# Scaling the last token tile on another engine, writing it by an accumulating store, and moving two multiplications and two weight loads

## The chip, the cores and the metric

The kernel runs on one core of one Trainium2 chip. The metric is the device time of one execution in microseconds (us); lower is better.

## What is computed

One layer of a diffusion backbone over 512 latent tokens of width 1024, with 256 context tokens. Only the part around the change has to be followed:

```python
x = x + g1 * mixed                                   # attention done before
hx2 = modulate(rmsnorm(x, norm_ffn_g[l]), sh2, sc2)  # h * (1 + scale) + shift
x = x + g2 * hierarchical_moe(hx2, ...)              # top-1 group, top-2 experts of it, 16 experts
return rmsnorm(x, final_norm_g)
```

So a row of `hx2` is `x * rstd * gs + sh`, where `rstd` is one number for each token, `gs = (1 + scale) * norm_ffn_g` and `sh` one vector each for all tokens. The router takes its logits from `hx2`; each token then goes through two of sixteen experts (`w_gate`, `w_up`, `w_down`), whose weights are 96 MB in all.

## The kernel before

The 512 tokens are four tiles of 128 rows (`t` = 0 to 3). After attention, each tile goes through the same steps:

- `out_sums` (L1217): TensorE multiplies by the output projection, in halves of 512 columns.
- `rows_half` (L1228): VectorE adds the residual (L1235); ScalarE squares and sums (L1237); VectorE multiplies by `gs` into `h2s[t]` (L1238). The buffers of `h2s` have the tag `t1`, of which there are three; the first held a constant, so tile 3 writes into the buffer of tile 0 and has to wait until tile 0's store has landed.
- `turn_half` (L1240): TensorE transposes four blocks; ScalarE copies them out of PSUM (L1246).
- `factor` (L1248) makes `rstd` in four small steps on VectorE and a root on ScalarE (L97 to L110), and `tile_logits` (L1253) the router's logits.
- `tile_end` (L1256): VectorE computes `h2s * rstd + sh` over 128x1024 (L1257), and SyncE (SP) issues the store of those rows to `hx_d` in DRAM (L1258).

`route` (L1108) is a generator of router steps on VectorE. `before3` is its instance for tiles 0 to 2 and `last3` the one for tile 3; `next(before3)` puts one step into VectorE's order. Its last steps, `places` (L1186), make the one-hot matrix `oh` for the slots: for tiles 0 to 2 by six instructions on GpSimd (POOL, L1192), for tile 3 by one on VectorE (L1195). `slot_sums` (L1199) multiplies them on TensorE; `slot_rows` (L1205) turns the result into the index list `idx`. Then `gather(0)` (L1260), an indirect DMA issued by GpSimd, fetches expert 0's token rows from `hx_d` into `xg[0]`; it needs `idx` and all four stores to `hx_d`. While it is under way VectorE computes the gains (`shares`, L1161), TensorE makes the other slot sums, and every engine passes a branch for overfull experts (L1415), whose body is not entered here. With `xg[0]` there, `turn_x(0)` transposes it (L1519), `split` makes `xh` (L62), and the matmuls of the sixteen experts follow without a gap.

Order. Inside `with tc.manual_schedule(engines=...)` (L1285) the named engines keep the order of the program; there these are TensorE and VectorE. The other engines' instructions are put in order by the framework's own list scheduler, which may move an instruction far ahead: the two `memset`s of `xg` (L1303), written inside the block, run on GpSimd at 368 us.

Weight loads. `load_experts(n)` (L446) issues the next n loads of 1 MB on SP. A load waits for the landing of the second load before it, or, where `behind` is given, for that instruction's landing alone. In the block one load is issued ahead of `tile_end(3)` and one behind it (L1325 to L1327). The loads up to the 15th wait for `gather(0)` (L1353), those after for `gather(1)` (L1493).

Of the kernel before, what the change touches and what calls it, by code (L numbers as in the profile page):

```python
# [12 lines left out]
AF = mybir.ActivationFunctionType  # L13
OP = mybir.AluOpType
# [3 lines left out]
P = 128  # L18
# [20 lines left out]
def hybrid_kernel(tc, nc, x_k, x_q, ctx, cvec, w_mod_a, w_mod_b, b_mod_c, b_mod_r, g_ffn_row,  # L39
                  w_v, w_kv, w_ql, w_qk, g_q, g_kv, w_uq, w_ukv, rel, w_out_a, w_out_b, w_r, b_r,  # L40
                  w_gate, w_up, w_down, g_fin_row, cpk0, cpk, out):
    sy, ac, ve, pe, gp = nc.sync, nc.scalar, nc.vector, nc.tensor, nc.gpsimd

    def pool(name, bufs=1, side="left", space=None):
        kw = dict(name=name, bufs=bufs, reuse_waits="tile")
        if space is None:
            return tc.alloc_tile_pool(side=side, **kw)
        return tc.alloc_tile_pool(space=space, **kw)
# [158 lines left out]
    def bank4(*nums):  # L207
        return bank(*nums).rearrange("p (a b) -> p a b", a=4)
# [143 lines left out]
    for b in range(3):  # L352
        n = KB[b + 1] - KB[b]
# [41 lines left out]
    for c in range(2):  # L395
        for b0, n in ((0, 4), (4, 2)):
            tr = bank4(4, 5, 6)
# [7 lines left out]
    for b0, n in ((0, 4), (4, 2)):  # L405
        tr = bank4(4, 5, 6)
# [10 lines left out]
    for c in range(3):  # L417
        tr = bank4(4, 5, 6)
# [22 lines left out]
    def add_slots(pl_, n):  # L441
        slots_.extend((pl_, f"ew{len(slots_) + i}") for i in range(n))
# [3 lines left out]
    def load_experts(n, behind=None):  # L446

        for i in range(len(loads), min(len(loads) + n, len(order))):
            e, q = order[i]
            pl_, tag = slots_[cur[0] % len(slots_)]  # L450
            cur[0] += 1
            places_.append(cur[0] - 1)
            w = pl_.tile([P, 2048], F32, name="ew", tag=tag, bufs=1)
            ins = sy.dma_start(w, (w_gate, w_up, w_down)[q // 2][e, q % 2])

            n_ = 2 if i < FL else FLIGHT
            if behind or i >= n_:
                tc.add_manual_dep(ins.ins, behind or started[i - n_], mybir.DependencyInfo(
                    mybir.DependencyClass.Sync, mybir.DependencyReason.DATA), reason="in flight")
            started.append(ins.ins.name)  # L460
            loads.append(w)
# [359 lines left out]
    def tr_tile():  # L821
        return psC.tile([P, 4, P], F32, name="tr", tag="tr", bufs=2)
# [257 lines left out]
    gs = wp.tile([P, D], F32, name="gs")  # L1080
    sh = wp.tile([P, D], F32, name="sh")
# [6 lines left out]
    load_experts(M1 - R1 - LD)  # L1088
    ve.scalar_tensor_tensor(gs, gs, 1.0, gff, op0=OP.add, op1=OP.mult)
    hx_d = tc.dram_tile([T, D], F32, name="hx_d")  # L1090

    def logits(ht):

        pl_ = psC.tile([P, 4, P], F32, name="o", tag="o", bufs=1)
        for k in range(KT):
            pe.matmul(pl_[:, 0, 0:20], ht[:, k, :], wr[:, k, :], start=(k == 0), stop=(k == KT - 1))
        return pl_[:, 0, 0:20]
# [7 lines left out]
    h2s = []  # L1105
# [93 lines left out]
    def slot_sums(pq, oh, va, i, n_i, n_rows):  # L1199

        for n in range(8):
            pe.matmul(pq[0:n_rows, 0, i * NE:(i + n_i) * NE], oh[n], va[n][:, i:i + n_i].rearrange("p a e -> p (a e)"),
                      start=(n == 0), stop=(n == 7))

    def slot_rows(pq, idx_, n_rows):  # L1205
        ve.tensor_scalar(idx_[0:n_rows, 0, :], pq[0:n_rows, 0, 0:NE], float(T), None, op0=OP.add)
# [10 lines left out]
    def out_sums(t, hf, cs_=range(4)):  # L1217
        if t not in ys_:
            ys_[t] = halves(0)
        cs = slice(hf * 512, hf * 512 + 512)  # L1220
        for c in cs_:
            wh, wl = wos[c]
            mm3(ys_[t][hf], omh[:, c, t * P:(t + 1) * P], oml[:, c, t * P:(t + 1) * P], wh[:, cs], wl[:, cs],
                start=(c == 0), stop=(c == 3))

    sq, hts = {}, {}

    def rows_half(t, hf):  # L1228

        if hf == 0:  # L1230
            sq[t] = wp.tile([P, 2], F32, name="ssh", tag="ssh", bufs=2)
            h2s.append(wp.tile([P, D], F32, name="t1", tag="t1", bufs=3))
        cs = slice(hf * 512, hf * 512 + 512)
        xs = x1s[t][:, cs]
        ve.tensor_tensor(xs, xs, ys_[t][hf], op=OP.add)  # L1235
        junk = wp.tile([P, 512], BF16, name="junk", tag="junk", bufs=2)
        ac.activation(junk, xs, AF.Square, accum_out=sq[t][:, hf:hf + 1])  # L1237
        ve.tensor_tensor(h2s[t][:, cs], xs, gs[:, cs], op=OP.mult)  # L1238

    def turn_half(t, hf):  # L1240
        if hf == 0:
            hts[t] = wp.tile([P, KT, P], F32, name="ht", tag="ht", bufs=1)
        tr = tr_tile()
        for k in range(4):
            pe.transpose(tr[:, k, :], x1s[t][:, (hf * 4 + k) * P:(hf * 4 + k + 1) * P], ident)
        ac.copy(hts[t][:, hf * 4:hf * 4 + 4, :], tr)  # L1246

    def factor(t):  # L1248
        ss = wp.tile([P, 1], F32, name="ss", tag="ss", bufs=2)
        yield from rstd_steps(ss, sq[t][:, 1:2], D, 1, wp, sq[t][:, 0:1])  # L1250
        yield ss

    def tile_logits(t, l, ss):  # L1253
        ve.scalar_tensor_tensor(lg[:, t, :], l, ss, lsh, op0=OP.mult, op1=OP.add)

    def tile_end(t, ss):  # L1256
        ve.scalar_tensor_tensor(h2s[t], h2s[t], ss, sh, op0=OP.mult, op1=OP.add)  # L1257
        return sy.dma_start(hx_d[t * P:(t + 1) * P, :], h2s[t]).ins.name  # L1258

    def gather(e):  # L1260
        ins = gp.indirect_dma_start(out=xg[e % NX][slice(0, CAP), :], out_offset=None, in_=hx_d,  # L1261
                                    in_offset=bass.IndirectOffsetOnAxis(ap=idx[slice(0, CAP), 0, e:e + 1], axis=0),
                                    bounds_check=T - 1, oob_is_err=False)
        gathers.append(ins.ins.name)
# [3 lines left out]
    for t in range(2):  # L1268
        out_sums(t + 1, 0)
        out_sums(t + 1, 1)  # L1270
        rows_half(t, 0)
        rows_half(t, 1)
        turn_half(t, 0)
        turn_half(t, 1)
        *_, ss = factor(t)
        tile_logits(t, logits(hts[t]), ss)
        tile_end(t, ss)

    N1, NF, N2 = 1, 3, 2
    L1, L2 = 2, 2  # L1280
# [1 line left out]
    R4 = 2  # L1282
    pp3 = pq0[:, 3:4, :]
    before3, last3 = route(0, 3), route(3, 4)
    with tc.manual_schedule(engines={pe.engine, ve.engine}):  # L1285
        out_sums(3, 0)
        rows_half(2, 0)
        rows_half(2, 1)
        turn_half(2, 0)
        turn_half(2, 1)  # L1290
        *_, ss = factor(2)
        out_sums(3, 1, (0, 1))
        tile_end(2, ss)
        l = logits(hts[2])
        rows_half(3, 0)
        out_sums(3, 1, (2, 3))
        ona.release()
        omp.release()
        chp.release()
        xp = pool("xp")  # L1300
        xg = [xp.tile([P, D], F32, name=f"xg{i}") for i in range(NX)]
        for x_ in xg:
            gp.memset(x_, 0.0)  # L1303
        rng4 = pool("rng4")
        add_slots(rng4, 5)
        rng5 = pool("rng5")
        add_slots(rng5, R4)
        vq = pool("vq")
        oh = vq.tile([P, 8, CAP], F32R, name="oh")
        va = vq.tile([P, 8, 4, NE], F32R, name="va")  # L1310
        pos = vq.tile([P, 4, 2], F32, name="pos")
        aa = vq.tile([P, 4, 2, 4, 4], F32, name="aa")
        aall = aa.rearrange("p t a g i -> p (t a) (g i)")
        load_experts(L1)
        tile_logits(2, l, ss)
        for _ in range(N1):
            next(before3)
        rows_half(3, 1)
        turn_half(3, 0)
        turn_half(3, 1)  # L1320
        for n, s3 in enumerate(factor(3)):
            if n < NF:
                next(before3)
        l = logits(hts[3])
        load_experts(L2 - 1)  # L1325
        tile_end(3, s3)
        load_experts(1)  # L1327
        for _ in range(N2):
            next(before3)
        tile_logits(3, l, s3)  # L1330
        for _ in before3:
            pass
        for _ in last3:
            pass
        slot_sums(pq0, [oh[:, n] for n in range(8)], [va[:, n] for n in range(8)], 0, 1, CAP)
        slot_rows(pq0, idx, CAP)
        gather(0)
        pc = tr_tile()
        for t in range(4):
            pe.matmul(pc[:, 0, 0:NE], trb[:, 1, :], mh[:, t, :], start=(t == 0), stop=(t == 3))  # L1340
        count = cst.tile([P, NE + 1 + NB * NE], I32, name="count")
        ve.tensor_copy(count[:, 0:NE], pc[:, 0, 0:NE])
        ve.tensor_reduce(out=count[:, NE:NE + 1], in_=pc[:, 0, 0:NE], axis=AX.X, op=OP.max)
        shares()
# [314 lines left out]
    with tc.manual_schedule(engines={pe.engine, ve.engine, ac.engine}):  # L1659
# [19 lines left out]
        for n in range(8):  # L1679
            wh, wl = half(n)  # L1680
            for i in range(2):
                k = n % 4 * 2 + i
                cs = slice(i * 512, i * 512 + 512)
# [235 lines left out]
```

## Time and profile before

| | |
|---|---|
| device time, three runs | 733.8, 735.29, 735.91 us; median 735.29 |
| the profiled execution | 733.54 us |
| its span, first to last instruction | 731.8 us |
| TensorE busy | 698.1 us, 95% of the span |
| VectorE, ScalarE, GpSimd busy | 546.4, 447.7, 83.7 us |
| granted TensorE clock, mean | 0.983 of full |

All rows of the trace are from the one profiled execution; its times count from the first instruction. "Start, length, engine, line, operation, written tile, read tiles" is the order within a row, and what stands in brackets is how long the engine had been idle and what ended that. Lines are those of the kernel before.

### The profile page before, as it was taken

How to read it: one execution, taken by the hardware profiler on the slowest of the kernel's cores; microseconds unless marked ns; L12 is line 12 of the kernel's file. 1: busy time of each engine (PE TensorE's matmuls, PEld its weight loads, DVE VectorE, ACT ScalarE, POOL GpSimd, SP SyncE). 2: the span in 40 equal slices, each digit the busy share in tenths (PEclk: the TensorE clock that was granted, in tenths of full speed). 3: DMA queues.
4: the chain of work that ended last, by engine and by line, in shares of the span. 5: the costliest groups of instructions: out<-in, count | busy, mean ns of one | idle time of the engine just before them, and what ended most of it. 6: DMA issues, size and time to landing. Idle time of an engine off the chain costs nothing. (4 is left out here: it accounts for less than half of the span.)

```text
span 731.8 us, 10466 instructions
## 1 busy us (share of the span) xinstructions
PE 698.1 (95%) x3918; PEld 516.9 (71%) x3919; DVE 546.4 (75%) x749; ACT 447.7 (61%) x698; POOL 83.7 (11%) x56
## 2 busy tenths in 40 slices
PE   4999999999999999999999679999999999999995
PEld 3678997767765887868658557777777777777773
DVE  4572457766676795656536778999999999999996
ACT  6451355654555455646644377777777777777763
POOL 1010000000000000000010122222222222221310
PEclk9999999999999999999999769999999999999998
DMA  8931238555476821121179979999999999999673
GB/s 319 409 124 60 73 95 279 194 172 190 144 236 202 288 88 43 60 76 54 59 252 364 346 244 364 362 372 370 353 360 357 358 352 350 358 354 379 239 132 116
DMA packets 39336, 174.58 MB, mean 239 GB/s; under 512 B 5711, under 2 KB 7191, under 8 KB 26992
## 3 DMA queue, kind: packets, MB, share of 16 engines
q1 hardware_dynamic: 34880, 163.72, 61.4%
q0 software_dynamic: 4112, 10.06, 6.3%
q8 instruction: 32, 0.52, 0.3%
q14 instruction: 24, 0.20, 0.1%
q10 hardware_dynamic: 288, 0.08, 0.0%
HBM read 163.00 MB, written 14.79 MB: 243 GB/s over the span
## 5 line engine op out<-in xcount | busy, mean ns | idle before, releaser
L1376 DVE TENSOR_TENSOR el<-ew,eh 128x2048 fp32r<-128x2048 f32 (+1 forms) x106 | 220.6, 2087 | 17.3 <-ACT eh L1373 13.7
L1373 ACT CAST eh<-ew 128x1024 fp32r<-128x1024 f32 x190 | 190.1, 1050 | 43.9 <-PE s L59 29.4
L57 PE MATMUL s<-eh,xh 128*96 128x512 f32 x260 | 104.7, 403 | 1.1 <-ACT xh L62 1.1
L59 PE MATMUL s<-eh,xl 128*96 128x512 f32 x260 | 103.3, 397 | 0.0
L58 PE MATMUL s<-el,xh 128*96 128x512 f32 x260 | 102.8, 395 | 0.0
L1588 POOL DMA_INDIRECT ya_d<-yo,idx x14 | 45.5, 3251 | 140.7 <-DVE yo L1592 140.7
L59 PEld LDWEIGHTS s<-eh,xl 128*96 128x96 f32 x260 | 42.3, 163 | 19.3 <-DVE xl L63 0.7
L57 PEld LDWEIGHTS s<-eh,xh 128*96 128x96 f32 x260 | 42.4, 163 | 18.3 <-ACT xh L62 1.4
L58 PEld LDWEIGHTS s<-el,xh 128*96 128x96 f32 x260 | 42.5, 164 | 17.5 <-DVE el L1376 0.2
L57 PE MATMUL y<-eh,ghh 128*96 128x512 f32 x120 | 48.2, 401 | 0.0
L59 PE MATMUL y<-eh,ghl 128*96 128x512 f32 x120 | 47.3, 394 | 0.0
L58 PE MATMUL y<-el,ghh 128*96 128x512 f32 x120 | 47.2, 393 | 0.0
L470 DVE TENSOR_REDUCE nm<-s 128x1 f32<-128x768 f32 x32 | 30.5, 954 | 19.1 <-PE s L59 18.9
L57 PE MATMUL ps<-wh,hh 128*128 128x512 f32 (+2 forms) x128 | 43.9, 345 | 0.5 <-ACT hh L275 0.3
L59 PE MATMUL ps<-wh,hl 128*128 128x512 f32 (+2 forms) x128 | 43.5, 345 | 0.2 <-DVE hl L277 0.2
L58 PE MATMUL ps<-wl,hh 128*128 128x512 f32 (+2 forms) x128 | 43.4, 341 | 0.0
L1303 POOL MEMSET xg<- 128x1024 f32 x2 | 1.9, 954 | 322.1 <-DMA g<-mod_d 322.1
L57 PE MATMUL ps<-hh,wh 128*128 128x512 f32 (+1 forms) x96 | 36.4, 379 | 0.0
L946 ACT ACTIVATE pr<-s,nm 128x768 f32<-128x768 f32 x32 | 29.1, 908 | 9.8 <-DVE nm L470 9.6
L59 PE MATMUL ps<-hh,wl 128*128 128x512 f32 (+1 forms) x96 | 34.4, 359 | 0.0
L58 PE MATMUL ps<-hl,wh 128*128 128x512 f32 (+1 forms) x96 | 34.2, 357 | 0.0
L1261 POOL DMA_INDIRECT xg<-hx_d,idx x16 | 24.2, 1510 | 65.9 <-PE t L1519 46.7
(360 smaller groups left out, 1455.8 us busy)
## 6 DMA issues: line engine op xcount, KB each, us to landing
ew<-w_gate SPq DMA_DIRECT2D x32, 1024.0 KB, 8.6
ew<-w_up SPq DMA_DIRECT2D x32, 1024.0 KB, 8.0
ew<-w_down SPq DMA_DIRECT2D x32, 1024.0 KB, 9.4
raw<-w_mod_b SPq DMA_DIRECT2D x32, 512.0 KB, 3.8
wm<-w_mod_a SPq DMA_DIRECT2D x16, 512.0 KB, 10.8
raw<-w_qk SPq DMA_DIRECT2D x8, 512.0 KB, 3.4
raw<-w_v SPq DMA_DIRECT2D x4, 512.0 KB, 10.5
ya_d<-zero SPq DMA_DIRECT2D x8, 256.0 KB, 3.2
```

Of the source, the lines that this page charges most:

```text
L57: pe.matmul(ps, lh, rh, start=start, stop=False)
L58: pe.matmul(ps, lh, rl, start=False, stop=False)
L59: pe.matmul(ps, ll, rh, start=False, stop=stop)
L470: ve.tensor_reduce(out=nm, in_=s, axis=AX.X, op=OP.max, negate=True)
L946: ac.activation(pr, s, AF.Exp, bias=nm, accum_out=mla_ssum[h // 2][:, t, h % 2:h % 2 + 1])
L1261: ins = gp.indirect_dma_start(out=xg[e % NX][slice(0, CAP), :], out_offset=None, in_=hx_d, in_offset=bass.IndirectOffsetOnAxis(ap=idx[slic ...
L1303: gp.memset(x_, 0.0)
L1373: ac.copy(wh[:, cs], r[:, cs])
L1376: ve.tensor_tensor(wl[:, cs], r[:, cs], f(wh[:, cs]), op=OP.subtract)
L1588: gp.indirect_dma_start(out=ya_d, out_offset=bass.IndirectOffsetOnAxis(ap=idx[rows, 1, e:e + 1], axis=0), in_=yo[rows, :], in_offset=None, ...
```

## The change

1. `tile_end(3)` no longer runs on VectorE. ScalarE multiplies `h2s[3]` by `rstd` (an activation of kind Copy with a scale for each row, 128x1024), and GpSimd issues a DMA that adds the result onto what stands in `hx_d`.
2. What stands there is `sh`: a new store on SP writes `sh` into those 128 rows of `hx_d`, soon after `sh` is loaded.
3. The two multiplications by `gs` of tile 3 move from VectorE to GpSimd.
4. GpSimd joins the engines that keep the order of the program in the block. Its order there is: multiplication of the first half, the two `memset`s of `xg`, multiplication of the second half, the accumulating store, the six `oh` instructions, `gather(0)`.
5. The copy out of PSUM for the second half of tile 3's transposes moves from ScalarE to VectorE. One step of `before3` moves ahead of it, and two steps instead of three stand between the steps of `factor(3)`.
6. Instead of one weight load ahead of `tile_end(3)` and one after it, one load is issued, and it waits for the accumulating store's landing. The other joins the load that waits for `gather(0)`.

```diff
     hx_d = tc.dram_tile([T, D], F32, name="hx_d")
+    sy.dma_start(hx_d[3 * P:4 * P, :], sh)
...
-        ve.tensor_tensor(h2s[t][:, cs], xs, gs[:, cs], op=OP.mult)
+        (ve if t < 3 else gp).tensor_tensor(h2s[t][:, cs], xs, gs[:, cs], op=OP.mult)
...
-        ac.copy(hts[t][:, hf * 4:hf * 4 + 4, :], tr)
+        if t == 3 and hf:
+            ve.tensor_copy(hts[t][:, hf * 4:hf * 4 + 4, :], tr)
+        else:
+            ac.copy(hts[t][:, hf * 4:hf * 4 + 4, :], tr)
...
     def tile_end(t, ss):
+        if t == 3:
+
+            ac.activation(h2s[t], h2s[t], AF.Copy, scale=ss)
+            return gp.dma_start(hx_d[t * P:(t + 1) * P, :], h2s[t], accum_op=OP.add).ins.name
...
-    with tc.manual_schedule(engines={pe.engine, ve.engine}):
+    with tc.manual_schedule(engines={pe.engine, ve.engine, gp.engine}):
...
         turn_half(3, 0)
+        next(before3)
         turn_half(3, 1)
         for n, s3 in enumerate(factor(3)):
-            if n < NF:
+            if n < NF - 1:
                 next(before3)
         l = logits(hts[3])
-        load_experts(L2 - 1)
-        tile_end(3, s3)
-        load_experts(1)
+        load_experts(1, tile_end(3, s3))
```

`NF` is 3 and `L2` is 2.

## Rows read from the trace of the kernel before

**Rows 1.** First line; stretches: length, PE, PEld, DVE, ACT, POOL busy, clock, DMA share, GB/s

```profile
span 731.8 us, 10466 instructions
...
387.00:398.00 11.00, 11.00 (x63) 9.41 (x63) 10.09 (x25) 5.63 (x13) 0.00 (x0) 1.00 0.98 366
412.70:425.00 12.30, 3.87 (x30) 3.34 (x31) 7.62 (x38) 4.67 (x6) 4.42 (x8) 0.50 0.81 278
457.00:690.00 233.00, 233.00 (x1109) 165.73 (x1108) 221.08 (x142) 179.47 (x199) 58.80 (x24) 1.00 0.99 359
```

**Rows 2.** Timeline of VectorE, 407 to 416 us

```profile
407.28 0.69 DVE L1238 TENSOR_TENSOR t<-x,gs 128x512 f32<-128x512 f32 x1 [0.72 <-DMA hx_d<-t]
...
409.05 0.69 DVE L1235 TENSOR_TENSOR x<-x,s 128x512 f32<-128x512 f32 x1 [0.16 <-PE s L59]
...
410.38 0.15 DVE L97 TENSOR_SCALAR nww<-ssh 128x1 f32<-128x1 f32 x1
...
412.24 1.28 DVE L1257 SCALAR_TENSOR_TENSOR t<-t,ss,sh 128x1024 f32<-128x1024 f32 x1
...
414.94 0.25 DVE L1153 TENSOR_REDUCE pos<-pm 128x6 f32<-128x96 f32 x1
```

**Rows 3.** Timeline of GpSimd, and its queue's waits and landing of gather(0) (L1261)

```profile
415.38 3.30 POOL L1192 TENSOR_SCALAR oh<-ck,pos 128x96 fp32r<-128x96 f32 x6 [44.90 <-DVE pos L1153]
...
420.82 1.09 POOL L1261 DMA_INDIRECT xg<-hx_d,idx  x1 [2.14 <-DVE ex L1166]
...
L1261 POOLq EVENT_SEMAPHORE  x4: 17/901/4222, 415.6 to 422.3; - x4
...
DMA to landing us min/median/max: 4.1/4.1/4.1
```

**Rows 4.** Timeline, the steps from the index list to the experts' first matmul

```profile
419.42 0.17 DVE L1206 TENSOR_SCALAR idx<-x 96x16 int32<-96x16 f32 x1 [1.13 <-PE x L1202]
...
424.39 0.65 PE L1202 MATMUL x<-va,oh 128*96 128x48 f32 x3 [0.30 <-PEq L1415]
...
425.02 1.51 PE L1519 MATMUL t<-c,xg 96*128 96x96 f32 x8
...
426.83 0.78 ACT L62 CAST xh<-t 128x768 fp32r<-128x768 f32 x1
```

**Rows 5.** Timeline of SP's issues, 412 to 425 us

```profile
412.75 0.33 SPq L454 DMA_DIRECT2D ew<-w_up  x1
413.55 0.33 SPq L1258 DMA_DIRECT2D hx_d<-t  x1
415.20 0.33 SPq L454 DMA_DIRECT2D ew<-w_up  x1
424.91 0.34 SPq L454 DMA_DIRECT2D ew<-w_down  x1
```

**Rows 6.** Gather(1): its issue, its landing, and queues' packets and MB, 426:429, then 429:431.8

```profile
424.96 1.01 POOL L1261 DMA_INDIRECT xg<-hx_d,idx  x1 [3.05 <-DMA xg<-hx_d,idx]
...
DMA to landing us min/median/max: 6.8/6.8/6.8
...
q1 hardware_dynamic: 122, 0.95, 85.9%
q0 software_dynamic: 5, 0.02, 1.7%
...
q0 software_dynamic: 209, 0.51, 68.4%
```

**Rows 7.** Prices: two groups of GpSimd, landing of L1640's accumulating transfers, a pass of ScalarE

```profile
L1640 POOL DMA_DIRECT2D x<-ya_d x4 | 3.7, 1436 | 4.5 <-ACT eh L1373 4.5
L1303 POOL MEMSET xg<- 128x1024 f32 x2 | 1.9, 954 | 322.1 <-DMA g<-mod_d 322.1
...
DMA to landing us min/median/max: 5.6/8.4/11.3
...
L1373 ACT CAST eh<-ew 128x1024 fp32r<-128x1024 f32 x190 | 190.1, 1050 | 43.9 <-PE s L59 29.4
```

## The prediction

> **What bounds the kernel now.** I read the busy time by stretch first [rows 1]. From 457 to 690 us TensorE is busy for all of 233.00 us: whatever moves the start of the experts' matmuls moves the end by as much, and nothing behind it hides a delay. From 412.7 to 425 us TensorE has 3.87 us of work in 12.3 us at half the full clock: the routing of the last tile and the fetch of expert 0's rows, where the change lies. The profiled execution took 733.54 us for a span of 731.8, 1.75 us below the median of 735.29; I work out a shift on the profiled one and add it to the median.
>
> The timelines of that stretch show two strands. One is **VectorE's**: tile 3's residual sum at 409.05, the factor's steps from 410.38, `tile_end` for 1.28 us at 412.24, the positions ready at 415.19 [rows 2]; then GpSimd's six `oh` instructions, 3.30 us from 415.38 to 418.68 [rows 3], and the index list at 419.42 to 419.59, 0.74 us after GpSimd's last [rows 4]. The other is the **store** of tile 3's rows, issued at 413.55 between two weight loads [rows 5]. `gather(0)` needs both. GpSimd's queue waited 4.222 us, from 415.7 (just after the first of those events at 415.6), to 419.9, 0.3 us beyond the index list: the store came last, by that little. The gather's own row starts at 420.82, 0.9 us after the wait, and it lands 4.1 us later, at 424.9 [rows 3]. The transposes of `xg` start at 425.02, just as TensorE ends the other slot sums (424.39 + 0.65); `xh` follows at 426.83 [rows 4]. So both strands end within 0.2 us of each other, and a gain has to come in both.
>
> **The change, part by part.**
>
> *VectorE.* It loses two multiplications (0.69 us as in the row at 407.28) and `tile_end` (1.28), and gets a copy of 128x512 out of PSUM, which I price as the sum that reads PSUM in the same shape, 0.69 [rows 2]. Between the sum's end at 409.74 and `rstd` at 412.24 it then has as much to do as before: the multiplication goes, the copy comes, and the three route steps stay (one of them moves ahead of the copy). But the copy has to wait for TensorE's transposes, which wait for the sum themselves, and the moved step fills only part of that wait. I allow 0.4 us for the rest, an estimate between nothing and the 0.7 of a whole half-tile operation. So `rstd` is ready at about 412.65, but `tile_end` doesn't follow it: the positions, 2.95 us after `rstd` before (412.24 to 415.19), come 1.67 us after it, at about 414.35, 0.85 earlier.
>
> *GpSimd's multiplications.* The first waits, as VectorE did, for tile 0's store (407.28 [rows 2]). No row shows a product of two inputs on this engine. From below: a `memset` writes 1024 columns in 0.954 us, so 512 written take 0.48 [rows 7]; from above: an `oh` instruction takes 0.55 us for 96 columns (3.30 / 6 [rows 3]), which times 512/96 is 2.9, as if nothing of it were fixed. I take 1.25, nearer the `memset`, since it has length and width like the product, with two operands read besides. The GPSIMD Engine Reference of the Trainium skill (section 3.1) gives 4497 ns for such an addition of 2048 columns, from which an estimate for 512 is 1.12 us; by it the sum stays as it is. With 1.25 us each and the two `memset`s between (1.9 [rows 7]) GpSimd ends at 407.3 + 4.4 = 411.7, ahead of `rstd`. This costs nothing up to (412.65 - 407.3 - 1.9) / 2 = 1.7 us each. The cover is 0.95 us.
>
> *ScalarE* scales 128x1024 in the time of a copy of that shape, 1.05 us [rows 7]: 412.7 to 413.8. It is otherwise idle here.
>
> *The store's issue on GpSimd.* It stands ahead of the six `oh` in the fixed order: a wait for ScalarE here would hold them up, and with them the index list. Four accumulating transfers issued in a row (L1640) kept GpSimd busy for 3.7 us, 0.92 each [rows 7]: 413.85 to 414.8, against positions at 414.35. So `oh` runs from 414.8 to 418.1, 0.6 earlier than before, and the index list is there at about 419.0.
>
> *The store's landing.* The first of the L1640 transfers, of the same 512 KB but from DRAM into SBUF, landed 5.6 us after its start, the others later as they queued behind each other (median 8.4) [rows 7]. From below I take the gather's 4.1 [rows 3], from above the 8.4. I take 5.6, as the store is alone once the earlier loads are through: 413.85 + 5.6 = 419.45. Before, the wait ended at 419.9, so here 0.45 us is won.
>
> *Storing `sh` first* adds 0.5 MB to a stretch with DMA at 0.98 share and 366 GB/s [rows 1]: 1.4 us of transfer time. The loads there are wanted after 427 us, so that costs nothing in itself; but tile 0's store, and with it GpSimd's first product, may come up to 1.4 us later. The cover of 0.95 us takes most of that; 0.45 us stays as a bound.
>
> *The weight loads.* The one of 415.20 goes behind the gather, with the one that was issued there at 424.91 [rows 5]; both feed chunks far behind, and I put that at nothing. The one of 412.75 now starts at the store's landing, 419.5, so right ahead of `gather(0)`. For that there is a model in the trace: at 424.91 a load was issued on SP, and at 424.96 `gather(1)` started [rows 5, 6]. From 426 to 429 us the load's queue moved 0.95 MB and the gather's 0.02; from 429 to 431.8 the gather's moved 0.51. The gather landed after 6.8 us instead of 4.1 [rows 6]. The load was through 4.1 us after its issue (429 less 424.91), and the gather landed 2.75 us after that (431.75). Here the load is through at 419.5 + 4.1 = 423.6, and `gather(0)` lands at 426.35. Alone it would have landed 4.1 us after its start at 419.45 + 0.9 = 420.35, so at 424.45.
>
> *The sum.* The transposes start at 426.4 instead of 425.02 and `xh` 1.6 us after that, at 428.0 (before, 1.81 passed there, the last 0.3 beyond the end of the transposes, waiting for work of VectorE that now comes earlier). That is 1.1 us behind 426.83 [rows 4]: 734.6 us for the profiled execution, **736.4** for the median. About 0.3% (2.2 us) is what a measurement of this kernel can tell from no change; I expect a loss below that. With the store's landing taken at 4.1 us the load is through at 422.1 and the gather lands at 424.85: no change. With 8.4 all shifts by another 2.8 us: 3.9 us slower.
>
> **The rivals.**
>
> *The gather isn't held up, and the time falls.* It then lands at 424.45, and TensorE's other slot sums end 0.6 earlier too, at 424.4. Both strands gain, `xh` comes 0.6 us earlier: 734.7. For it: the load starts 0.9 us ahead of the gather's row, and a queue could have let the gather in between; against it, the 0.02 MB from 426 to 429 us [rows 6]. The page DMA: Bandwidth & Descriptors of the Trainium skill (section on queues, rings and completion order) says that each DMA engine goes round between the queues packet by packet; by that rule the gather would share the bandwidth and this rival would hold, and the trace does not agree in the one stretch that resembles it. A quarter.
>
> *GpSimd is too slow, and the time rises clearly.* It hangs on one number, the product's duration, and decides from 1.7 us on. At 2.9 us: 407.3 + 2.9 + 1.9 + 2.9 = 415.0; ScalarE ends at 416.2; the store lands at 416.25 + 5.6 = 421.85; the load behind it is through at 426.0, the gather lands at 428.75, and the shift is 3.5 us: 738.8. For it: the fixed order puts everything behind these products. The same page on GpSimd (section 8) says that the engine contends with VectorE's instructions of two inputs for SBUF; VectorE runs those all through this stretch. Against it: the spread of 0.48 to 2.9 lies mostly below 1.7 where the width of the `memset` counts. 15 in 100.
>
> *Nothing changes.* The store lands early (as with 4.1 above), or the two effects cancel, and what VectorE loses was not on the path, since GpSimd's `oh` waits for the store's issue: within 0.7 us of 735.3. 15 in 100.
>
> **How the numbers follow.** Forecast (736.4) 45 in 100, rivals 25, 15 and 15. The forecast's own range, from the landing's bounds, is 735.3 to 739.2, most of it below 737.5. Faster than 733.1 is only the far end of the first rival, and what I have not seen: 9 in 100. Slower than 737.5: the second rival with 15 and the forecast's tail with 7, so 22. Within: 69. The range of 8 in 10 reaches from 733.6, a little beyond the first rival, to 738.2, where most of the second is left out.
>
> **What the profile after would show.** The load behind the store between the landing and the gather, its bytes first, and a landing of `gather(0)` over 5 us: the forecast. A landing near 4 us: the first rival. GpSimd's products over 1.7 us, or ScalarE's scaling starting later than `rstd`: the second. Positions by 414.5 and the index list by 419.1 would show VectorE's part right. The forecast is wrong if the store lands much before 419, if SP's order moves other stores, or if the start of the experts' matmuls moves without moving the end.

## The result and the profile after

The changed kernel takes **740.73 us** (median of 6 executions, 738.92 to 743.45) beside 733.15 us for the kernel before (6 executions, 732.35 to 735.91). The ratio is **1.0090, 95% interval 1.0067 to 1.0114**: 6.6 us slower. Forecast were 736.4 us, a range up to 738.2 and no change that can be measured; the time lies above the range. The profiled execution after took 740.42 us, that of before 733.54; their spans differ by 6.8 us.

The first line of the page, and the busy time by stretch with the columns of [rows 1], one stretch added:

```profile
span 738.6 us, 10459 instructions
...
387.00:398.00 11.00, 11.00 (x64) 9.42 (x63) 10.08 (x25) 5.62 (x13) 0.00 (x0) 1.00 0.97 364
412.70:425.00 12.30, 3.44 (x31) 2.95 (x30) 8.44 (x40) 5.87 (x6) 6.22 (x9) 0.58 0.65 187
425.00:446.00 21.00, 14.77 (x51) 9.55 (x51) 11.38 (x12) 8.78 (x10) 2.56 (x2) 0.68 0.77 279
457.00:690.00 233.00, 233.00 (x1109) 165.71 (x1108) 220.22 (x135) 178.98 (x198) 60.19 (x25) 1.00 1.00 364
```

From 387 to 398 us and from 457 to 690 us TensorE, its clock and the engines' work are those of [rows 1]. The loss lies between: from 425 to 446 us TensorE is busy for 14.77 us. The same stretch of the kernel before:

```profile
425.00:446.00 21.00, 19.88 (x82) 13.72 (x82) 17.28 (x17) 14.96 (x19) 4.98 (x3) 0.80 0.86 298
```

There it was busy for 19.88 us, with 82 instructions in place of 51. The steps that lead there, in the timeline of the changed kernel, put together from GpSimd, VectorE, ScalarE and TensorE (start, length, engine, line, operation, then the idle time before it and what ended it):

```profile
409.59 1.27 POOL L1239 TENSOR_TENSOR t<-x,gs 128x512 f32<-128x512 f32 x1 [362.69 <-DMA hx_d<-t]
...
415.61 0.92 POOL L1264 DMA_DIRECT2D hx_d<-t  x1 [1.75 <-ACT t L1263]
...
421.84 1.07 POOL L1269 DMA_INDIRECT xg<-hx_d,idx  x1 [2.25 <-DVE e L1172]
```

```profile
409.71 1.42 DVE L1124 TENSOR_TENSOR eq<-eq,ck 128x240 f32<-128x240 f32 x1
...
412.79 1.09 DVE L105 SCALAR_TENSOR_TENSOR nwv<-nwv,nwr 128x1 f32<-128x1 f32 x1
...
420.33 0.17 DVE L1207 TENSOR_SCALAR idx<-x 96x16 int32<-96x16 f32 x1 [1.18 <-PE x L1203]
```

```profile
414.16 1.15 ACT L1263 ACTIVATE t<-t,ss 128x1024 f32<-128x1024 f32 x1 [1.98 <-DVE gsel L1132]
...
429.22 0.80 ACT L62 CAST xh<-t 128x768 fp32r<-128x768 f32 x1 [2.86 <-PE t L1526]
436.76 5.78 ACT L1380 CAST eh<-ew 128x1024 fp32r<-128x1024 f32 x6 [6.74 <-SPq L1422]
```

```profile
427.67 1.51 PE L1526 MATMUL t<-c,xg 96*128 96x96 f32 x8 [2.18 <-DMA xg<-hx_d,idx]
430.07 0.74 PE L57 MATMUL s<-eh,xh 128*96 128x512 f32 x1 [0.89 <-ACT xh L62]
...
437.86 0.48 PE L57 MATMUL s<-eh,xh 128*96 128x512 f32 x1 [2.38 <-ACT eh L1380]
439.12 0.74 PE L58 MATMUL s<-el,xh 128*96 128x512 f32 x1 [0.78 <-DVE el L1383]
```

The same two steps, ScalarE's cast of chunk 1 and the experts' first matmul, in the kernel before:

```profile
427.51 2.94 ACT L1373 CAST eh<-ew 128x1024 fp32r<-128x1024 f32 x3
```

```profile
427.66 0.74 PE L57 MATMUL s<-eh,xh 128*96 128x512 f32 x1 [1.12 <-ACT xh L62]
```

**First loss.** The experts' first matmul starts at 430.07; before it started at 427.66, 0.83 us behind the `xh` of [rows 4]. That is 2.4 us: the gather starts 1.0 us later than in [rows 3] and takes 5.7 us to land in place of 4.1.

**Second loss, not foreseen.** Behind chunk 0 (one chunk is one load, twelve matmuls here) TensorE stands still for 2.38 and then 0.78 us, since ScalarE's cast of chunk 1 begins only at 436.76. Its data had landed long before (the first weight loads are issued at 241 us). What the cast waits for is SP's queue at L1422, the overflow branch. In the kernel before nothing stood still here. From the first matmul to the next transposes of `xg` it is 15.8 us (430.07 to 445.83) in place of 11.1 (427.66 to 438.74): 4.7 more, of which the two stops are 3.2. The other 1.5 goes for the most part with the clock: 17 of the 36 matmuls took 0.63 us or more, before it were 12. Behind the stops the granted clock is 0.60 (437.8 to 441.5, matmuls of 0.63 us), where before it was 1.00 from 433.5 on.

Why SP is late is seen in its queue's instructions on the line of the branch (durations min/median/max, first and last start). Before, then after:

```profile
L1415 SPq EVENT_SEMAPHORE  x9: 17/17/17, 420.9 to 422.7; - x9
...
L1415 SPq COMPARE_BRANCH  x1: 50/50/50, 420.4 to 420.4; - x1
```

```profile
L1422 SPq EVENT_SEMAPHORE  x9: 17/17/17, 429.6 to 436.7; - x9
...
L1422 SPq COMPARE_BRANCH  x1: 50/50/50, 429.1 to 429.1; - x1
...
  ACT eh L1380: 6.7, 1
```

Where the branch's body is not entered, SP goes through nine semaphore instructions that stand in for it. Each waits for a count of one semaphore and then adds to it; eight of these semaphores are ones that DMAs add to when they land. I read them as keeping the counts as the body's own DMAs would have left them. Before, SP was through at 422.7, ahead of the load that waits for `gather(0)` ([rows 5], 424.91); it had stood for 1.3 us at the semaphore of the load issued at 415.20. After, both loads behind the gather stand ahead of the branch on SP:

```profile
421.04 6.88 SPq L454 DMA_DIRECT2D ew<-w_up  x2
427.98 9.52 SPq L454 DMA_DIRECT2D ew<-w_down  x2
```

(a row covers several issues: `w_up` at 421.04 and 427.60, `w_down` at 427.98, and one more at 437.16 behind the branch). SP comes to the branch at 429.1 with two loads in flight. It passes the fourth of the nine, on the semaphore of the load of 427.60, at 432.18, and the fifth, on that of the load of 427.98, at 436.44; it leaves at 436.7. ScalarE's cast of chunk 1 takes a buffer which the body borrows for its own weights, and so waits for one of the counts that SP adds at the end.

### The profile page after: what moved, and what is told of

Its sections match the earlier page's. It is cut to its first block, busy times and chain, and to the rows that moved or that the text cites. A ratio compares the mean times of both kernels' runs of the same rounds, so it can differ in the third digit from the quotient of the medians.

```text
span 738.6 us, 10459 instructions
## 1 busy us (share of the span) xinstructions
PE 699.6 (95%) x3918; PEld 517.5 (70%) x3919; DVE 547.1 (74%) x747; ACT 446.2 (60%) x697; POOL 86.5 (12%) x59
## 5 line engine op out<-in xcount | busy, mean ns | idle before, releaser
L1239 POOL TENSOR_TENSOR t<-x,gs 128x512 f32<-128x512 f32 x2 | 2.5, 1263 | 362.7 <-DMA hx_d<-t 362.7
L470 DVE TENSOR_REDUCE nm<-s 128x1 f32<-128x768 f32 x32 | 30.5, 954 | 19.2 <-PE s L59 18.9
```

The costliest lines, as they stand in the source:

```text
L470: ve.tensor_reduce(out=nm, in_=s, axis=AX.X, op=OP.max, negate=True)
L1239: (ve if t < 3 else gp).tensor_tensor(h2s[t][:, cs], xs, gs[:, cs], op=OP.mult)
```

## The experiments

All ratios are to the kernel before, measured beside it on the same chip. The profiled executions reach this stretch up to 3.5 us apart, so the table counts from **A**, the start of tile 3's first residual sum. "Index list" is the start of the instruction that writes `idx`. "Gather" is the start of `gather(0)` and the start of the transposes of `xg`; "SP through" is the last of the nine instructions. Loads issued more than 1.5 us ahead of the gather are not counted; in the kernel before the last 0.26 MB of the load of 415.20 still fall into the gather's first microsecond. Each line is of one profiled execution; the ratio is of all.

| kernel | loads beside the first gather / between it and the branch | index list | gather | first matmul | SP through | cast of chunk 1 | ratio (95%) |
|---|---|---|---|---|---|---|---|
| before | 0 / 0 | 13.6 | 15.0, 19.2 | 21.8 | 16.8 | 21.6 | 1 |
| changed | 1 / 2 | 14.4 | 15.9, 21.8 | 24.2 | 30.8 | 30.8 | 1.0090 (1.0067-1.0114) |
| e1 | 1 / 0 | 13.1 | 14.8, 21.0 | 23.4 | 19.9 | 23.3 | 0.9993 (0.9976-1.0010) |
| e2 | 1 / 1 | 13.3 | 14.9, 20.9 | 23.3 | 28.9 | 28.9 | 1.0068 (1.0042-1.0094) |
| e3 | 0 / 1 | 13.1 | 14.5, 19.1 | 21.9 | 24.4 | 24.4 | 1.0017 (0.9997-1.0036) |
| e4 | 1 / 1 | 13.5 | 14.6, 22.5 | 25.0 | 28.1 | 28.1 | 1.0040 (1.0023-1.0058) |
| e5 | 0 / 1 | 14.2 | 17.9, 22.9 | 25.4 | 30.5 | 30.5 | 1.0015 (0.9993-1.0036) |
| e6 | 1 / 0 | 13.2 | 14.9, 20.8 | 23.2 | 20.0 | 23.0 | 0.9981 (0.9965-0.9997) |
| e7 | 0 / 0 | 13.9 | 15.3, 20.0 | 22.8 | 16.5 | 22.7 | 0.9989 (0.9968-1.0010) |
| e8 | 1 / 0 | 13.5 | 14.6, 22.3 | 24.8 | 21.6 | 24.6 | 1.0016 (0.9992-1.0039) |
| e9 | 1 / 2 | 13.3 | 14.5, 20.4 | 22.8 | 30.5 | 22.7 | 1.0067 (1.0044-1.0090) |
| e10 | 0 / 0 | 13.3 | 14.9, 19.4 | 22.1 | 16.1 | 22.0 | 0.9967 (0.9951-0.9983) |
| e11 | 0 / 2 | 15.5 | 16.8, 22.3 | 24.7 | 31.0 | 31.0 | 1.0068 (1.0040-1.0097) |
| e12 | 0 / 0 | 14.8 | 15.8, 20.8 | 23.6 | 17.1 | 23.5 | 0.9986 (0.9967-1.0004) |

**e1, one line moved.**

```diff
-    load_experts(BO - len(loads), gathers[0])
...
     overflow()
+    load_experts(BO - len(loads), gathers[0])
```

> The changed kernel with one line moved: the call that issues the two loads behind the gather stands in the program behind the overflow branch, so SP passes the branch before it issues them, as in the kernel before. Theory (the branch cost most): in the changed kernel SP came to the branch with both loads in flight and stayed in it until they had landed, at 436.44, and ScalarE's cast of chunk 1 began at 436.76. With the branch ahead of the loads the cast starts at about 430, the time falls by about 4.4 us, from 740.7 to some 736.3 (735.5 to 737.5), and what is left over the kernel before is the 2.4 us by which the experts' first matmul started late. Rival (the late first part is all of it, and the branch only shows it): the time stays at 740 or above.

734.48 us, ratio 0.9993: not 4.4 but all of the 6.6 us come back. SP's queue and ScalarE in this kernel:

```profile
L1421 SPq EVENT_SEMAPHORE  x9: 2/17/17, 421.5 to 425.9; - x9
```

```profile
429.30 3.89 ACT L1379 CAST eh<-ew 128x1024 fp32r<-128x1024 f32 x4
```

The cast follows `xh` at once. That the whole loss goes has two reasons: the late index list of the changed kernel's profile belongs to that execution (below), and in this execution what is left of the late start weighs half. Counted from A the first matmul starts 1.6 us later than before, but the clock rises at A + 27.5 in both (0.39 us a matmul from 433.49 here, from 433.41 before). So four matmuls move from the slow part into the fast one, 4 x 0.23 = 0.9 us, and from A to the end this execution is 0.85 us longer than that of before.

**e2, the products back on VectorE.**

```diff
-        (ve if t < 3 else gp).tensor_tensor(h2s[t][:, cs], xs, gs[:, cs], op=OP.mult)
+        ve.tensor_tensor(h2s[t][:, cs], xs, gs[:, cs], op=OP.mult)
```

> The changed kernel with the norm-weight products of the last tile back on VectorE; the rest of the change stays, but one load alone is left ahead of the overflow branch, so that the branch is expected to cost about what it does with the call moved. Theory (VectorE stood still beside GpSimd's products): eq*tj goes back from 1.42 to 0.40 us and the sum of squares' instruction from 1.09 to 0.21, two products of about 0.6 us come onto VectorE, and the route's index list is ready about 0.5 to 1 us earlier than 420.33. The time would be 0.5 to 1 us under that of the kernel with the branch moved, so about 735.5 (734.5 to 736.5). Rival (GpSimd's late products are the whole loss of the first part): as the kernel before, 733.3. Rival (they cost nothing): as the kernel with the branch moved, 736.3.

738.79 us, ratio 1.0068: a miss, but not of the products. I had taken the one load that stays ahead of the branch for harmless. SP is through at A + 28.9, and TensorE stands still again:

```profile
437.77 0.48 PE L57 MATMUL s<-eh,xh 128*96 128x512 f32 x1 [1.49 <-ACT eh L1380]
439.03 0.63 PE L58 MATMUL s<-el,xh 128*96 128x512 f32 x1 [0.78 <-DVE el L1383]
```

**e3, no load behind the store.** e1's edit, and

```diff
-        load_experts(1, tile_end(3, s3))
+        tile_end(3, s3)
```

> The changed kernel with the call moved behind the branch and without the load behind the accumulating store: all three of these loads wait for the gather. Theory (the load's packets go ahead of the gather's): the first gather takes about 4.1 us from issue to landing in place of 5.8, the matmuls of the experts start 1.7 us earlier, and the time is about 734.6 (733.8 to 735.5), if the load that starts later is not late itself. Rival (the gather is not held up by the load, and is late by the store alone): the landing stays at 5.5 us or more and the time at that of the kernel with the branch moved, 736.3.

736.05 us, ratio 1.0017, above the expectation. The gather takes 4.7 us to its transposes and the first matmul is 1.5 us earlier than in e1, as expected; but one of the three loads came to stand ahead of the branch, SP is through only at A + 24.4, and a stop of 0.88 us follows later.

**e4, the loads' order in the kernel before.**

```diff
-        load_experts(L2 - 1)
-        tile_end(3, s3)
-        load_experts(1)
+        load_experts(1, tile_end(3, s3))
```

> The kernel before with only the order of the loads changed: no load is issued ahead of the last tile's store and one behind it, in place of one behind it and one ahead, and two are left behind the gather. Theory (the branch among the loads costs, wherever it comes behind a load): SP comes to the branch with loads in flight and waits for their landing; if both are ahead of it the time is 3 to 4.5 us above that of the kernel before, 736.5 to 738; if one alone is, under 1 us, 733.2 to 734.2. Rival (the order of the loads costs nothing without the late store): 733.3 within 0.3%.

737.25 us, ratio 1.0040, where I expected under 1 us with one load ahead of the branch: a miss. Two costs are mixed here: the gather took 8.0 us until its transposes, and SP was through at A + 28.1.

From here SP's order is fixed by hand, so that each cost can be had alone: `with tc.manual_schedule(engines={sy.engine}):` around `overflow()` and the call of `load_experts`, in the order wanted.

**e5, the branch late in the kernel before.**

```diff
-    load_experts(BO - len(loads), gathers[0])
...
-    overflow()
+    with tc.manual_schedule(engines={sy.engine}):
+        load_experts(BO - len(loads), gathers[0])
+        overflow()
```

> The kernel before with one thing changed: SP issues its load behind the gather ahead of the overflow branch instead of behind it, by a fixed order of SP's instructions; the other engines then put all their slot sums and casts of chunk 0 ahead of their own branch, as in the changed kernel. No operation is added or taken away, and the last tile's end is that of the kernel before. Theory (the branch's place among the loads is what the change really cost): SP comes to the branch at about 425.4 with a load in flight, stays until it has landed at about 434, ScalarE's cast of chunk 1 starts then in place of 429.4, TensorE stands still for 2 to 3 us more and stays longer at the lower clock: 3 to 5 us slower than the kernel before, 737.3 to 739.3 beside 734.3. Rival (the late branch costs only because the changed kernel's gather and loads are late): within 0.3% of the kernel before.

735.99 us, ratio 1.0015: 1 us where I expected 3 to 5. Eight of ten executions took 733.9 to 736.9 us, two 740.2 and 741.1. The profile is of the slowest. The waits of GpSimd's queue ahead of its first gather there:

```profile
L1261 POOLq EVENT_SEMAPHORE  x3: 17/43/6576, 417.1 to 423.8; - x3
```

It waited 6.6 us, to 423.8, though the list was ready at 421.1: the last store was late, the gather started at A + 17.9, SP was through at A + 30.5, and TensorE stood still for 1.34 and 0.79 us. The first matmul is 3.6 us later behind A than in the kernel before, so what this execution loses is not the order's alone: more than half of it comes with the late store. In the eight the order costs little. Of them there is no profile; e3, with one load ahead of the branch and a gather in time, shows what they may look like.

**e6, e1's order with the products on VectorE** (e2's edit, and the two loads behind the branch).

> The changed kernel with the two loads behind the gather held behind the overflow branch by a fixed order of SP's instructions, and the last tile's norm-weight products on VectorE. To be read against the run with the call moved, 0.9993 of the kernel before, which has them on GpSimd. Theory now: there GpSimd's products began right behind their sums, at 407.18, and the index list was ready 13.1 us behind the first sum of the last tile (14.4 in the changed kernel's profile, where tile 0's buffer came free late in that execution). On VectorE they take about 1.3 us of it and take away as much standing still: the list is ready 13.1 to 13.4 us behind that sum and the time is the same as with them on GpSimd, within 0.3% (733.8 to 734.8 beside 734.3). Rival (GpSimd's products cost the route 1 us or more): 733.3 or less.

734.46 us, ratio 0.9981. The time alone looks as expected, but the kernel before took 734.97 beside it, and by the ratio this is 1.4 us faster, on the rival's side. The list is as late as in e1 (13.2 and 13.1), and the interval overlaps that of e1 (0.9993): a difference between GpSimd and VectorE is not shown. e10 against e7 below points the same way, also within the intervals, so a cost of 1 to 2 us is not excluded either.

**e7, nothing ahead of gather and branch** (e3's edit, and all three loads behind the branch).

> The changed kernel with all three loads held behind the overflow branch by a fixed order of SP's instructions, so that none stands ahead of the first gather and SP goes through the branch with no load in flight. Theory (a load's packets ahead of the gather's hold it up by 1.5 to 2 us, and half of that is given back because TensorE's clock rises at the same time): the gather takes about 4.5 us in place of 6.2, the experts' first matmul starts some 21.9 us behind the first sum of the last tile in place of 23.4, SP leaves the branch within 3 us of its start, and the time is about 0.8 us under that of the run with the call moved, 733.5 (732.5 to 734.3). Rival (the gather is late by itself): no difference to the run with the call moved.

733.46 us, ratio 0.9989, inside the range; but that is only 0.3 us under e1, less than either interval, so the times don't part theory and rival. The trace does: gather to transposes is 4.7 us in place of 6.2, and SP is through 1.3 us behind its branch. The first matmul comes at A + 22.8 and not at 21.9, since the list was later here (13.9).

**e8, e4 with the branch early.**

> The kernel before with the change's order of the loads alone (none ahead of the last tile's store, one behind it), and SP's order fixed so that the two loads behind the gather come behind the branch. In the run without that fixed order, 1.004 of the kernel before, the gather took 8 us. Theory (two separate costs: the load beside the gather, and loads ahead of the branch): the gather still takes 6 to 8 us and the experts' first matmul starts 1.5 to 3 us later than in the kernel before, half of which is given back; ScalarE's cast of chunk 1 is not held by SP any more; 0.5 to 1.5 us slower than the kernel before, 734.8 to 735.8 beside 734.3. Rival (all of the 0.4% is the load beside the gather): 1.004 again, 737.2.

736.92 us, ratio 1.0016, 1.2 us, inside the expectation by the ratio. But the executions fall into two groups: seven took 736.7 to 738.3 us, much as e4's, and three 733.3 to 733.7. The interval overlaps that of e4 (1.0023 to 1.0058), so how much of e4's loss is the branch is not shown. The profile is of one of the seven: no stop is left, the gather takes 7.8 us until the transposes, and both the first matmul and the end come about 3 us later behind A than in the kernel before (3.0 and 3.2). There the late gather costs its full length; in e1 no cost can be measured.

**e9, the body borrows one buffer fewer.** The order is the changed kernel's. The body of the branch, not entered with these inputs, passes its weights through one cast buffer in turn (its loads and second product are put in order for that):

```diff
-        wx = [ep.tile([P, 2048], F32, name="wx", tag="eh", bufs=3) for i in range(2)]
+        wx = [ep.tile([P, 2048], F32, name="wx", tag="eh", bufs=3)] * 2
```

> The changed kernel in its own order, branch behind the loads as there. Only the overflow branch's body is changed, which these inputs do not enter: its weights go through one of the three cast buffers in turn, not through two, so that ScalarE's cast of chunk 1 takes a buffer that the branch has not borrowed, and the cast of chunk 2 is the first that has to wait until SP has left the branch. No instruction outside the body changes. Theory (what costs is that the next cast must wait for SP to stand in for the branch's own loads): SP leaves the branch late as before, some 30.5 us behind the first sum of the last tile, but the cast of chunk 1 starts right behind xh, at about 24.5 us in place of 30.8; TensorE does not stand still behind chunk 0, and at most 1 us behind chunk 1; the time falls by 3 to 5 us from 740.7, to 736 to 738 (1.002 to 1.005 of the kernel before). Rival (the late loads themselves, or the other engines' order round the branch, are the cost): the time stays at 1.008 or above.

```profile
427.00 1.99 ACT L1380 CAST eh<-ew 128x1024 fp32r<-128x1024 f32 x2
434.87 5.78 ACT L1380 CAST eh<-ew 128x1024 fp32r<-128x1024 f32 x6 [5.88 <-SPq L1422]
```

```profile
435.97 0.47 PE L57 MATMUL s<-eh,xh 128*96 128x512 f32 x1 [0.59 <-ACT eh L1380]
439.24 0.74 PE L58 MATMUL s<-el,xh 128*96 128x512 f32 x1 [2.81 <-DVE el L1383]
```

739.35 us, ratio 1.0067, above the range; the interval overlaps that of the changed kernel, so the times don't show a gain. The trace shows where the stop comes from. The wait moved as the theory says: chunk 1 is cast at once (427.00), chunk 2 waits for SP (434.87). That shows the chain from SP's branch over the borrowed buffer to the cast. The size I had wrong: the stop comes a chunk later and is 3.4 us, because from chunk 2 on VectorE makes `el` in one piece of 2.29 us once both halves are cast.

**e10, all of it together:** e7's order and the products on VectorE.

> The best of the parts together: the changed kernel with SP's order fixed so that no load stands ahead of the first gather or of the overflow branch, and the last tile's products on VectorE; ScalarE scales the rows and the accumulating store adds them, as in the change. Theory: the index list is ready 13.2 us behind the first sum of the last tile in place of 13.55, the gather takes under 5 us, the experts' first matmul starts at 21.7 to 22.2 us and nothing stands still behind it; the time is 0.998 of the kernel before (0.996 to 1.000), that is 733 beside 734.5. Rival (nothing of the shorter VectorE chain reaches the gather, since the accumulating store's landing releases it): 1.000.

732.84 us (12 executions, 731.76 to 733.91), ratio **0.9967, interval 0.9951 to 0.9983**: faster than both kernels, by 2.4 us over the kernel before by the ratio. The fastest executions of both are alike (731.76 and 731.87 us beside it); but 15 of 23 of the kernel before took longer than the slowest of e10. So the gain lies in the longer executions that are missing, not in a faster best one; of what makes those longer there is no profile.

```profile
420.94 1.09 POOL L1269 DMA_INDIRECT xg<-hx_d,idx  x1 [2.35 <-DVE e L1172]
```

```profile
425.47 1.51 PE L1527 MATMUL t<-c,xg 96*128 96x96 f32 x8
428.18 0.74 PE L57 MATMUL s<-eh,xh 128*96 128x512 f32 x1 [1.20 <-ACT xh L62]
```

The start of the matmuls is no earlier than before (A + 22.1 and 21.8). In this profile the clock rises 3.3 us behind the first matmul in place of 5.8; whether that is the order's doing or this execution's was not tried.

**e11, two loads ahead of the branch, none ahead of the gather.**

```diff
+    with tc.manual_schedule(engines={sy.engine}):
+        load_experts(2, gathers[0])
+        overflow()
+        load_experts(BO - len(loads), gathers[0])
```

> As the run with no load ahead of the gather and the branch early (0.999 of the kernel before), but two of the three loads stand ahead of the overflow branch again, as in the changed kernel. So far the branch behind loads cost 0.7 to 0.9% where a load stood ahead of the gather too, and 0.15% where one load alone stood ahead of the branch and the gather was alone. Theory (only the landing of the last load ahead of the branch against the moment at which chunk 1 is wanted decides): the gather lands some 19 to 20 us behind the first sum of the last tile, SP leaves the branch about 9 us later, at 27.5 to 29; the cast of chunk 1 starts 1 to 3 us after TensorE has finished chunk 0; 2 to 5 us slower than with the branch early, 736.5 to 739 (1.003 to 1.006). Rival (the gather has to be late as well): within 0.2% of the kernel before.

```profile
436.27 5.79 ACT L1379 CAST eh<-ew 128x1024 fp32r<-128x1024 f32 x6 [6.38 <-SPq L1421]
```

```profile
437.37 0.47 PE L57 MATMUL s<-eh,xh 128*96 128x512 f32 x1 [2.30 <-ACT eh L1379]
```

739.65 us, ratio 1.0068: the theory holds, a little above its upper end. A load ahead of the gather is not needed; with two loads to wait for SP is late enough (A + 31.0). The profile is of the slowest of the seven executions (736.87 to 741.38), and its list is late too (15.5), which is part of its loss.

**e12, e10's order in the kernel before,** whose last tile's end stays on VectorE and SP.

> The kernel before with the order of the loads from the best run alone (0.9967): its last tile's end is untouched, on VectorE and SP; all three loads are held behind the overflow branch. Theory (the gain of the best run lies in the loads being out of the way of store, gather and branch): 0.997 to 0.999 of the kernel before. Rival (it lies in the change's own part, VectorE's chain without the scaling): 1.000 or above, since the loads start 10 us later here.

732.96 us, ratio 0.9986. The interval takes in 1 and overlaps that of e10. How much of e10's gain is the order, how much the shorter chain on VectorE and how much the products there stays open. The change as it was written, with its products on GpSimd, can be read against this run: e7 has the same order of the loads and 0.9989. Between the two no gain of the change's own idea is seen.

## Why the prediction was wrong

The step that failed is the one on the weight loads: "both feed chunks far behind, and I put that at nothing". For the chunks that they feed it holds. But they were moved on SP's queue, and what else stands on it I looked through for stores only. In the kernel before SP passes the overflow branch at 420.4 to 422.7, ahead of the load at 424.91. The rows of that line stood in the trace, and the branch is named in the text on the kernel. With two loads behind the gather the framework's scheduler put the branch behind them, the cast of chunk 1 hung on SP, and no rival had this. Put at nothing, it cost 4.7 us in the profile, and by the ratios the change without it is about 7 us faster: e1 (0.9993 in place of 1.0090) and e11 against e7 (1.0068 and 0.9989) show the cost in both directions, e9 the path that it takes. Why the scheduler chose that order was not tried.

The other steps, against e1, which has the forecast's path without the late branch:

- **VectorE.** Forecast: `rstd` at 412.65, positions at 414.35, list at 419.0. In e1: 412.9, 414.5 and 419.1. Right. In the changed kernel's profile all of it is 1.2 us later, since tile 0's buffer came free at 409.6.
- **GpSimd's products.** 1.25 us forecast, 1.28 and 1.27 measured; the rival at 2.9 us falls. They cost VectorE something that I left out (last section); whether they cost the kernel anything is open (e6).
- **ScalarE, the store's issue, `oh`, landing.** 1.15 us for 1.05; 0.92 as taken; six `oh` in 3.34; the landing 5.5 us for 5.6. Right.
- **Storing `sh` first.** No cost of it is seen in e1, whose first product starts at 407.18, as [rows 2] at 407.28. The 409.59 of the changed kernel's profile, A + 3.7, varies with the execution: e9, with the same order, has A + 1.2. In e12, which has no such store, VectorE waited for tile 0's store as well, to A + 3.0; the latest of all, A + 4.9, is e11, which has the store of `sh`. So that this store never delays tile 0's is not shown. The row of e12:

```profile
409.24 0.69 DVE L1238 TENSOR_TENSOR t<-x,gs 128x512 f32<-128x512 f32 x1 [2.29 <-DMA hx_d<-t]
```

- **The load beside the gather.** The mechanism was right. The queues' packets and MB in the changed kernel, from 422 to 425 us and then to 427.7:

```profile
q1 hardware_dynamic: 123, 1.01, 92.3%
...
q0 software_dynamic: 112, 0.33, 38.7%
q1 hardware_dynamic: 20, 0.03, 3.2%
```

  For three microseconds the load's queue alone moves, then the gather's. In e7, with no load beside it, the gather's queue moves in the same three microseconds of its way (419.75 to 422.75):

```profile
q0 software_dynamic: 92, 0.29, 36.6%
```

  So the gather waits behind the load's bytes. Forecast were 6.0 us from the gather's start to its landing; to the transposes it is 5.8 in the changed kernel and 6.2 in e1. The rival of a gather that is not held up falls. The prediction took the rule of packets in turn (Trainium skill, DMA: Bandwidth & Descriptors, section Queues, rings and completion order) to mean an even sharing, and the trace to be against it. That does not follow: the section gives some 9 to 17 descriptors for a typical packet, and the load's 1 MB goes in pieces of 8 KB (1.01 MB in 123), by an estimate 8 for each of the 16 DMA engines. So an engine's share of the load may be one packet, and no run here tests the rule.
- **From that to the time.** The forecast carried 1.1 us at full weight to the end. e1's first matmul is 1.6 us late behind A, its end 0.85 us, and the ratios put it at -0.5 us with an interval from -1.8 to 0.7. "Whatever moves the start moves the end by as much" is too strict: in e1 the clock rose no later than before, and a late start was partly given back. It is not always so: in e8 the clock rose at A + 31.0, and a start 3.0 us late made the end 3.2 us late.

Without the late branch the forecast of no measurable change would have stood; its 1.1 us lies just above e1's interval.

## What to carry to other kernels

When a DMA is moved on a queue, list every instruction of that queue between its old and its new place, branches first: an engine that passes a branch with DMAs in flight may stand there until they have landed, and whoever uses a buffer that the branch's body borrows stands with it. A transfer that nobody needs soon can be late for the queue behind it. And where an automatic order is left in place, compare the order of each engine before and after, since here the branch got another place among the instructions of VectorE, ScalarE and TensorE too.

## What the runs showed that I had not expected

- **VectorE stands still while GpSimd multiplies.** In the changed kernel `eq` took 1.42 us beside the product at 409.59, and a one-column step 1.09 us beside the product at 412.61; in e1 the same steps took 0.40 and 0.21 us, away from the products. Both read two inputs from SBUF, and the second ended with the product, at 413.9. During GpSimd's `memset`s such steps kept their usual 0.40. The Trainium skill says so (SBUF — State Buffer, section SBUF: two separate sides: a GpSimd instruction that reads SBUF and a VectorE instruction of two SBUF inputs exclude each other for the whole instruction), and the trace agrees.
- **A stop of TensorE can cost the clock as well.** Busy time by stretch in e2, ahead of its stops of 1.49 and 0.78 us, behind them, and further on (the clock is the third number from the end):

```profile
435.60:436.30 0.70, 0.68 (x3) 0.21 (x1) 0.00 (x0) 0.00 (x0) 0.00 (x0) 0.87 0.08 29
438.60:442.00 3.40, 2.97 (x7) 1.95 (x8) 2.92 (x3) 3.40 (x5) 0.00 (x0) 0.59 0.99 419
443.00:446.00 3.00, 3.00 (x14) 2.08 (x13) 2.81 (x2) 2.01 (x2) 0.00 (x0) 1.00 1.01 423
```

  The granted clock was rising, fell back to near 0.5 of full (1.2 of 2.4 GHz) behind the stops, and was full again from 443. The changed kernel shows the same (0.50 from 439.2 to 441.5 us), so these stops cost more than their own length. Not every stop does: ahead of e3's single stop of 0.88 us (433 to 437 us) and behind it (438 to 440) the clock is 1.00.
- **Executions of one kernel spread by several us.** With the branch late in the kernel before (e5), eight executions lay within 3 us and two 3 us above them; e8's fall into two groups 3 us apart, and the 31 of the kernel before beside them reach from 731.5 to 737.3. One profile shows one of them: in e5's a late store. So a profile explains its own execution, and the ratio of all has to bear it out.
